# Two feed-forwards and a grouped attention in 512-wide and side-by-side passes

## The chip, the cores and the metric

One core of one Trainium2 chip runs the whole program: two transformer-like blocks, the second with two layers. The metric is the device time of one execution in microseconds, lower is better. A profiled execution adds a trace of every engine: TensorE (PE, and PEld for its weight loads), VectorE (DVE), ScalarE (ACT), GpSimd (POOL) and the queue of SyncE (SP), which issues the transfers.

## What is computed

The parts of the reference that the change touches, cut from the rest (all in fp32; 256 tokens, width 1024, hidden width 2816):

```python
def swiglu(hn, w_gate, w_up, w_down):
    return (jax.nn.silu(hn @ w_gate) * (hn @ w_up)) @ w_down
...
h = h + swiglu(rms_norm(h, ffn_norm_g[i]), w_gate[i], w_up[i], w_down[i])
...
def gqa_attend(q, k, v):
    s = jnp.einsum("bhgqd,bhkd->bhgqk", q, k).astype(jnp.float32) * (HEAD_DIM ** -0.5)
    p = jax.nn.softmax(s, axis=-1).astype(v.dtype)
    return jnp.einsum("bhgqk,bhkd->bhgqd", p, v)
...
def swiglu_2(h, w1, w3, w2):
    return (jax.nn.silu(h @ w1) * (h @ w3)) @ w2
```

The first block ends with one feed-forward (`swiglu`) for 256 tokens. The second block has two layers with two streams of 256 tokens each, the latent one and the context. In layer 0 both streams go through the attention and the feed-forward, 512 tokens in all; in layer 1 only the latent stream does, 256 tokens. The grouped attention has 8 query heads of 64 channels and 2 key and value heads; the latent stream attends to 512 keys, the context to its own 256.

## The kernel before, in words

Activations lie with channels on the partitions and tokens along the free axis. To keep fp32 accuracy, each operand is split in a high part (rounded to fp32r) and a low part (the rest), and a product is three passes into one PSUM tile: high by high, high by low, low by high. `mm3` (L282) issues them at L288, L289 and L290; each pass is a MATMUL with a weight load (LDWEIGHTS) of its own.

```python
nc.tensor.matmul(ps, lhsT=l[0], rhs=r[0], start=start, stop=False)
nc.tensor.matmul(ps, lhsT=l[0], rhs=r[1], start=False, stop=False)
nc.tensor.matmul(ps, lhsT=l[1], rhs=r[0], start=False, stop=stop)
```

A k-tile here is one stationary tile of 128 x 128 with its low part, applied to all tokens of the operand: three passes of 256 columns where there are 256 tokens.

Weights come from HBM in blocks of 128 output channels. `wload` (L266) issues one transfer of 512 KB into `wr`, then ACT casts it to the high part `wh` (L277) and VectorE subtracts to get the low part `wl` (the helper's line, L250). Each of the three has three buffers. `proj_fm` (L292) walks over groups of blocks that fill one PSUM tile of 512 columns, so two blocks share a tile when there are 256 tokens; three PSUM tiles (`pp`) rotate. When a group is complete its `evac` function takes the sums out.

`swiglu` (L1136) runs gate and up projections in pairs of blocks. `ev_g` and `ev_u` work on 512 columns at a time: tanh on ACT, two products on VectorE, and a split of the result into the high and low pages `G`. Then the down projection runs over 22 k-tiles for each of 8 blocks. `ffn1` (L1190) is the first block's feed-forward. Its first two pairs of blocks (the lead) run on the unnormalised operand `hr` while the norm is still being computed, and the factor `rbs` is multiplied in afterwards; the rest runs on `hf_hi` and `hf_lo`. `ffn2` (L1634) is the feed-forward of the second block; its operand pages are `H`, high and low apart.

`gqa` (L1375) computes for each of 4 pairs of heads and each stream the scores, the softmax `e` on ACT and VectorE, transposes of `e` (`pT`, split into `pt_hi` and `pt_lo`) and the sums over keys. There the values of both value heads are one stationary tile (`vh`, and `vl` for the low part), and of the 128 rows that come out only the 64 of the head in question are used.

The order of the work is set when the program is built. A scheduler sorts the instructions of each engine into one fixed order, from their dependencies and from the order in which the generators are woven; each engine then runs its list strictly in that order. Beside the feed-forward of the first block runs `ada` (L1254): products of modulation weights on VectorE (`aj`), whose steps `run` and `fill` (L1216) hand out between steps of the projection. Beside the grouped attention run the gating of another branch (`merge`) and the convolution (`conv`, on VectorE, `cy`).

Of the kernel before, what the change touches and what calls it, by code (L numbers as in the profile page):

```python
# [10 lines left out]
F32 = mybir.dt.float32  # L11
# [11 lines left out]
NF = FF // 128  # L23
# [157 lines left out]
class Prog:  # L181
# [146 lines left out]
    @staticmethod  # L328
    def tail(n_tok):

        per = 512 // n_tok
        g = [[(n + j, 0, 0, n_tok) for j in range(per)] for n in range(0, 6, per)]
        return g + [[(n, 0, t, t + 256)] for t in range(0, n_tok, 256) for n in (6, 7)]

# [854 lines left out]

    def ffn1(self, h, st, before_down):  # L1190

        t = self.t
        g = self.v("ffn_g")
        raw = self.scaled(h, g, "hr")
        rb = self.rs_bcast(st)
        hn = self.page("hf_hi", F32R), self.page("hf_lo", F32R)
        for k in range(8):
            s = slice(k * 256, k * 256 + 256)
            self.norm_apply(h[:, s], rb, g[:, k:k + 1], hn[0][:, s], hn[1][:, s])
        self.hold()  # L1200
        rbs = self.t512("rbs", F32, "h")[:, :256]
        self.nc.scalar.copy(rbs, rb)
        st = self.stats()
        st2 = self.stats(share=st)
        ev = self.ev_add(h, 0.5, st, (st2, self.v("fin_g")))
        pages = lambda ti, x, n: [(self.xpage if x == 0 or i == 0 else self.page)("G", F32R) for i in range(n)]
        self.run(self.swiglu(t["w_gate"], t["w_up"], lambda ti: [(t["w_downa"], 8), (t["w_downb"], 6)],
                             self.k256(hn), 256, pages, lambda ti, *a: ev(*a), [list(range(NF))], (self.k256(raw), rbs),
                             before_down), 0.5)
        return st  # L1210

# [130 lines left out]
    def values(self, l, at, n):  # L1342

        nc = self.nc
# [4 lines left out]
        for tt in range(4):  # L1349
            c = slice(tt * 128, tt * 128 + 128)  # L1350
            nc.tensor.transpose(ps[:, c], vz[:, c], self.ident)
        v = [self.kvp.tile([128, 512], F32R, tag="v" + x, bufs=2, name="v" + x) for x in "hl"]
# [22 lines left out]
    def gqa(self, l, at, qs, branch):  # L1375
# [6 lines left out]
        for n in range(4):  # L1382
# [3 lines left out]
            for i in qs:  # L1386
# [247 lines left out]
    def ffn2(self, l, hs, sts):  # L1634
        t = self.t
        last = l == 1
        qs = [0] if last else [0, 1]
        nq = 256 * len(qs)
        with ExitStack() as es:
            if not last:  # L1640
                self.extra(es, 4)
                self.ada_tiles(es, 1024, 2)
                self.bg = _seq(self.ada(0, 5, [0, 1]), *[self.ada(1, x, [0, 1] if x < 2 else [0]) for x in range(6)])
# [6 lines left out]
            thirds = [list(range(NF))] if last else [list(range(8)), list(range(8, 16)), list(range(16, 22))]  # L1650
# [3 lines left out]
            if last:  # L1654
                down = lambda ti: [(t[f"w2{l}a"], 8), (t[f"w2{l}b"], 6)]
            else:
                down = lambda ti: [(t[f"w2{l}a"][:, ti:ti + 1], 8)] if ti < 2 else [(t[f"w2{l}b"], 6)]
# [155 lines left out]
```

## Time and profile before

| | |
|---|---|
| median of 3 runs (lowest to highest) | 2183.4 us (2180.99 to 2183.92) |
| the profiled execution | 2183.66 us |
| its span | 2181.4 us |
| TensorE busy in the span | 2102.3 us |
| VectorE busy in the span | 1660.8 us |
| ScalarE busy in the span | 867.1 us |
| mean granted clock of TensorE | 0.985 |

Busy time is the time in which an engine had at least one instruction running. TensorE's passes overlap, so the distance between the starts of two passes says more about their price than the duration of one. A stretch of the table by windows gives the busy time of each engine in it; the engine that is close to the length of the stretch is the short one there.

### The profile page before, as it was taken

How to read it: one execution, taken by the hardware profiler on the slowest of the kernel's cores; microseconds unless marked ns; L12 is line 12 of the kernel's file. 1: busy time of each engine (PE TensorE's matmuls, PEld its weight loads, DVE VectorE, ACT ScalarE, POOL GpSimd, SP SyncE). 2: the span in 40 equal slices, each digit the busy share in tenths (PEclk: the TensorE clock that was granted, in tenths of full speed). 3: DMA queues.
4: the chain of work that ended last, by engine and by line, in shares of the span. 5: the costliest groups of instructions: out<-in, count | busy, mean ns of one | idle time of the engine just before them, and what ended most of it. 6: DMA issues, size and time to landing. Idle time of an engine off the chain costs nothing. (4 is left out here: it accounts for less than half of the span.)

```text
span 2181.4 us, 34428 instructions
## 1 busy us (share of the span) xinstructions
PE 2102.3 (96%) x13408; PEld 1838.3 (84%) x13408; DVE 1660.8 (76%) x3401; ACT 867.1 (40%) x1379; POOL 68.8 (3%) x92
## 2 busy tenths in 40 slices
PE   8898999999998999999999999999999989999998
PEld 7677999999987777777788888878898868999998
DVE  8987775886579998888875899763499977666554
ACT  2223354545433445445433322222245444444442
POOL 2350000000000000000000000000000000000000
PEclk9999999999999999999999999999999989999999
DMA  6227654475642212333455367752344313364553
GB/s 225 85 76 232 210 183 145 152 236 179 188 141 73 84 59 92 112 126 121 141 173 189 99 217 224 260 185 97 93 147 142 101 43 103 129 201 155 184 182 127
DMA packets 97826, 322.20 MB, mean 148 GB/s; under 512 B 10496, under 2 KB 16128, under 8 KB 96768
## 3 DMA queue, kind: packets, MB, share of 16 engines
q1 hardware_dynamic: 97664, 320.01, 45.6%
q8 instruction: 105, 1.72, 0.3%
q14 instruction: 57, 0.47, 0.1%
HBM read 315.78 MB, written 4.19 MB: 147 GB/s over the span
## 5 line engine op out<-in xcount | busy, mean ns | idle before, releaser
L277 ACT CAST wh<-wr 128x1024 fp32r<-128x1024 f32 (+2 forms) x455 | 470.4, 1034 | 786.3 <-PE pp L289 552.8
L250 DVE TENSOR_TENSOR wl<-wr,wh 128x1024 fp32r<-128x1024 f32 (+2 forms) x455 | 546.8, 1202 | 222.7 <-ACT wh L277 217.0
L288 PE MATMUL pp<-H,wh 128*128 128x512 f32 (+1 forms) x1648 | 566.5, 346 | 7.0 <-ACT H L450 3.7
L289 PE MATMUL pp<-H,wh 128*128 128x512 f32 (+1 forms) x1648 | 565.5, 345 | 0.7 <-DVE H L253 0.7
L290 PE MATMUL pp<-H,wl 128*128 128x512 f32 (+1 forms) x1648 | 563.9, 344 | 1.0 <-DVE wl L250 0.8
L288 PEld LDWEIGHTS pp<-H,wh 128*128 128x128 f32 x1648 | 314.2, 191 | 44.1 <-ACT H L450 4.3
L290 PEld LDWEIGHTS pp<-H,wl 128*128 128x128 f32 x1648 | 313.7, 191 | 36.6 <-DVE wl L250 2.0
L289 PEld LDWEIGHTS pp<-H,wh 128*128 128x128 f32 x1648 | 313.9, 191 | 35.3 <-issue 2.7
L1267 DVE SCALAR_TENSOR_TENSOR aj<-aw,silu 128x512 f32<-128x512 f32 x320 | 220.2, 688 | 54.9 <-DMA aw<-ada 50.5
L288 PE MATMUL pp<-G,wh 128*128 128x256 f32 (+1 forms) x540 | 170.3, 315 | 0.0
L290 PE MATMUL pp<-G,wl 128*128 128x256 f32 (+1 forms) x540 | 170.3, 315 | 0.0
L289 PE MATMUL pp<-G,wh 128*128 128x256 f32 (+1 forms) x540 | 170.2, 315 | 0.0
L253 DVE SCALAR_TENSOR_TENSOR cy<-U,vecs,cy 128x512 f32<-128x512 f32 (+1 forms) x240 | 147.3, 614 | 2.6
L288 PEld LDWEIGHTS pp<-G,wh 128*128 128x128 f32 x540 | 103.0, 191 | 6.5
L289 PEld LDWEIGHTS pp<-G,wh 128*128 128x128 f32 x540 | 103.0, 191 | 6.4
L290 PEld LDWEIGHTS pp<-G,wl 128*128 128x128 f32 x540 | 103.0, 191 | 6.3
L289 PE MATMUL pp<-hf_lo,wh 128*128 128x256 f32 x320 | 90.7, 284 | 1.0 <-DVE hf_lo L250 0.9
L290 PE MATMUL pp<-hf_hi,wl 128*128 128x256 f32 x320 | 90.5, 283 | 1.0 <-DVE wl L250 1.0
L288 PE MATMUL pp<-hf_hi,wh 128*128 128x256 f32 x320 | 90.7, 284 | 0.3 <-ACT hf_hi L447 0.3
L253 DVE SCALAR_TENSOR_TENSOR h<-pp,mod,h 128x256 f32<-128x256 f32 x80 | 35.6, 479 | 65.3 <-PE pp L290 61.9
L286 PE MATMUL pp<-xg,wf 128*128 128x256 f32 x320 | 76.4, 392 | 9.3 <-DVE th L250 7.4
L1110 ACT ACTIVATE e<-sc,st 128x512 f32<-128x512 f32 (+1 forms) x104 | 62.3, 604 | 45.0 <-DVE st L257 29.1
(501 smaller groups left out, 3855.7 us busy)
## 6 DMA issues: line engine op xcount, KB each, us to landing
wr<-w SPq DMA_DIRECT2D x88, 512.0 KB
aw<-ada SPq DMA_DIRECT2D x72, 512.0 KB
wr<-zg SPq DMA_DIRECT2D x64, 512.0 KB
wr<-wb SPq DMA_DIRECT2D x48, 512.0 KB
aw<-ada SPq DMA_DIRECT2D x48, 256.0 KB
wr<-w_gate SPq DMA_DIRECT2D x22, 512.0 KB
wr<-w_up SPq DMA_DIRECT2D x22, 512.0 KB
wr<-w_downa SPq DMA_DIRECT2D x16, 512.0 KB
```

What stands on the lines that cost most here:

```text
L250: (eng or self.nc.vector).tensor_tensor(out=out, in0=a, in1=b, op=op)
L253: self.nc.vector.scalar_tensor_tensor(out, a, s, b, op0, op1)
L277: nc.scalar.copy(hi, raw)
L286: nc.tensor.matmul(ps, lhsT=l, rhs=r, start=start, stop=stop)
L288: nc.tensor.matmul(ps, lhsT=l[0], rhs=r[0], start=start, stop=False)
L289: nc.tensor.matmul(ps, lhsT=l[0], rhs=r[1], start=False, stop=False)
L290: nc.tensor.matmul(ps, lhsT=l[1], rhs=r[0], start=False, stop=stop)
L1110: nc.scalar.activation(e, ps[:, x], AF.Exp, bias=st[:, 2 + x:3 + x], scale=scale, accum_out=st[:, 4 + x:5 + x])
L1267: nc.vector.scalar_tensor_tensor(junk, w[:, c:c + 512], 1.0, self.sc[s][:, b + c:b + c + 512], MUL, MUL, accum_out=raw[i][:, (b + c) // 51 ...
```

## The change

It does three things.

First, `proj_wide` and `swiglu_wide` take the place of `proj_fm` and `swiglu` in the feed-forward of the first block and in the one of layer 1. High and low parts of the operand lie side by side, 256 columns each (`hpair`). A k-tile is then two passes: the high weights by all 512 columns, and the low weights by the first 256. One block fills a PSUM tile, high and low sums side by side, and `added` puts them together: ACT copies one half into `sm`, VectorE adds the other. Tanh and products follow on `sm`, 512 wide for two blocks, and the split goes into pages `G` in which high and low parts of a block lie side by side. In the down projection `ev_wide` adds the two halves to `h` one after the other. The steps of `ada` are handed out at half the rate per step, since there are twice as many steps.

Second, in `gqa` the high and low values of one head lie side by side in one stationary tile (`vg`), so that two passes, `pt_hi` and `pt_lo`, give the high sums in 64 rows and the low sums in the other 64. After them a copy on ACT and an addition on VectorE for each head put the two together in `go`, and one split writes both heads. The product of low values with low probabilities, which was left out before, is in the sums now.

Third, `values` writes the tiles for that in two splits of half the size.

```diff
+    def proj_wide(self, parts, rhs, evac, blocks=None):
+        nc = self.nc
+        nt = parts[0][0].shape[3] // parts[0][1] // 128
+        for c in range(parts[0][0].shape[0]) if blocks is None else blocks:
+            w = [self.wload(src[c, b], kc) for src, kc in parts for b in range(src.shape[1])]
+            ks = [x for (src, kc), x in zip([p for p in parts for b in range(p[0].shape[1])], w) for x in
+                  [(x[0][:, k], x[1][:, k]) for k in range(kc)]]
+            for j in range(nt):
+                s = slice(j * 128, j * 128 + 128)
+                ps = self.ps("pp")
+                last = len(ks) - 1
+                for k, (h, l) in enumerate(ks):
+                    r = rhs(k)
+                    if k:
+                        nc.tensor.matmul(ps[:, :256], lhsT=l[:, s], rhs=r[:, :256], start=False, stop=False)
+                    nc.tensor.matmul(ps, lhsT=h[:, s], rhs=r, start=k == 0, stop=k == last)
+                    if not k:
+                        nc.tensor.matmul(ps[:, :256], lhsT=l[:, s], rhs=r[:, :256], start=False, stop=False)
+                evac(c * nt + j, ps.rearrange("p (x n) -> p x n", x=2))
+                yield
...
+    def swiglu_wide(self, gate, up, down, rhs, page, ev_down, lead=None, before_down=None):
+        nc = self.nc
+        G = [page(i) for i in range(-(-NF // 4))]
+        sums = {}
+        def added(which, f, pv, rb):
+            if f % 2 == 0:
+                sums[which] = self.t512("sm", F32, "g")
+            x = sums[which][:, f % 2 * 256:f % 2 * 256 + 256]
+            nc.scalar.copy(x, pv[:, 1])
+            self.tt(x, pv[:, 0], x, ADD)
+            if rb is not None:
+                self.tt(x, x, rb, MUL)
+            return sums[which]
+        def ev_g(f, pv, rb=None):
+            x = added(0, f, pv, rb)
+            if f % 2:
+                th = self.t512("th", F32, "h")
+                nc.scalar.activation(th, x, AF.Tanh, scale=0.5)
+                self.stt(x, th, 1.0, x, ADD, MUL)
+        def ev_u(f, pv, rb=None):
+            x = added(1, f, pv, rb)
+            if f % 2:
+                self.tt(x, x, sums[0], MUL)
+                g = G[f // 4].rearrange("p (f x n) -> p x f n", f=4, x=2)[:, :, f % 4 - 1:f % 4 + 1]
+                self.split(x.rearrange("p (f n) -> p f n", f=2), g[:, 0], g[:, 1])
+        for f in range(0, NF, 2):
+            r, rb = lead if f == 0 and lead else (rhs, None)
+            yield from self.proj_wide([(gate, 8)], r, lambda *a: ev_g(*a, rb=rb), [f, f + 1])
+            yield from self.proj_wide([(up, 8)], r, lambda *a: ev_u(*a, rb=rb), [f, f + 1])
+        if before_down:
+            before_down()
+        yield from self.proj_wide(down, lambda k: G[k // 4][:, k % 4 * 512:k % 4 * 512 + 512], ev_down)
...
+    def ev_wide(self, h, scale, sts):
+        def ev(n, pv):
+            s = slice(n * 256, n * 256 + 256)
+            c = scale if isinstance(scale, float) else scale[:, n:n + 1]
+            for x in range(2):
+                self.stt(h[:, s], pv[:, x], c, h[:, s], MUL, ADD)
+            if n % 2 or n >= 6:
+                for st, g in sts:
+                    self.ssq_add(st, h[:, (n if n >= 6 else n - 1) * 256:(n + 1) * 256], g)
+        return ev
...
     def values(self, l, at, n):
...
+        if n == 0:
+            out = []
+            for a, x in enumerate("hl"):
+                v = self.kvp.tile([128, 512], F32R, tag="v" + x, bufs=2, name="vg")
+                v4 = v.rearrange("p (t j c) -> p t j c", t=2, j=4)
+                self.split(ps[:, a * 256:a * 256 + 256].rearrange("p (t j c) -> p t j c", t=2, j=2), v4[:, :, 0::3], v4[:, :, 1:3])
+                out += [[v[:, o:o + 128] for o in (t, t + 128)] for t in (0, 256)]
+            return out
...
     def gqa(self, l, at, qs, branch):
...
-                        self.mm3(ov[:, j], tuple(x[:, kt * 128:kt * 128 + 128] for x in gv),
-                                 pt[m], m == 0, m == nk // 128 - 1)
+                        for x in range(2):
+                            nc.tensor.matmul(ov[:, j], lhsT=gv[kt][j], rhs=pt[m][x], start=m == x == 0,
+                                             stop=m == nk // 128 - 1 and x == 1)
                     yield
+                o = self.t512("go", F32, "h")[:, :256]
+                for j in range(2):
+                    rows, other = [slice(64 * x, 64 * x + 64) for x in (j, 1 - j)]
+                    nc.scalar.copy(o[rows], ov[other, j])
+                    self.tt(o[rows], ov[rows, j], o[rows], ADD)
                 c = slice(n * nq + i * 256, n * nq + i * 256 + 256)
-                for j in range(2):
-                    rows = slice(64 * j, 64 * j + 64)
-                    self.split(ov[rows, j], branch[0][rows, c], branch[1][rows, c])
+                self.split(o, branch[0][:, c], branch[1][:, c])
```

The order in which the engines run the instructions changes at three places that matter here. The names are those of the program with the number of the buffer.

VectorE (DVE) in the first feed-forward, behind the lead. `aj` are products of `ada`, `wl` are low parts of weights. Before, the end of the first pair and the split of the weights of the fourth block behind the lead:

```order
L1267 SCALAR_TENSOR_TENSOR aj_4427,ar_4419<-aw_4421,silu0_1711 128x512
L250 TENSOR_TENSOR gu_4407<-th_4342,pp_4345 128x512
L1267 SCALAR_TENSOR_TENSOR aj_4429,ar_4420<-aw_4421,silu1_1721 128x512
L253 SCALAR_TENSOR_TENSOR th_4492<-th_4492,pp_4431 128x512
L250 TENSOR_TENSOR G_4276<-gu_4407,G_4273 128x512
L250 TENSOR_TENSOR wl_4529<-wr_4526,wh_4528 128x1024
```

And now (the sums `pp_4417`, `pp_4443` and `pp_4471` are the first three blocks behind the lead):

```order
L250 TENSOR_TENSOR sm_4358<-sm_4358,sm_4302 128x512
L1348 SCALAR_TENSOR_TENSOR aj_4409,ar_4400<-aw_4401,silu1_1721 128x512
L250 TENSOR_TENSOR sm_4434<-pp_4417,sm_4434 128x256
L250 TENSOR_TENSOR G_4273<-sm_4358,G_4273 128x2x256
L250 TENSOR_TENSOR sm_4434<-pp_4443,sm_4434 128x256
L250 TENSOR_TENSOR sm_4488<-pp_4471,sm_4488 128x256
L250 TENSOR_TENSOR wl_4494<-wr_4491,wh_4493 128x1024
```

Three additions stand ahead of the same split, `wl_4494`, where none stood.

ScalarE (ACT) at the start of the last feed-forward, behind the last piece of the operand `H`. Before:

```order
L450 ACTIVATE H_19467<-nx_19513,mod1_3_0_14411 128x256
L277 CAST wh_19620<-wr_19618 128x1024
L277 CAST wh_19655<-wr_19653 128x1024
L1155 ACTIVATE th_19584<-pp_19523 128x512
L277 CAST wh_19685<-wr_19683 128x1024
```

And now:

```order
L473 ACTIVATE H_19036<-nx_19081,mod1_3_0_14032 128x256
L1223 COPY sm_19114<-pp_19097 128x256
L277 CAST wh_19173<-wr_19171 128x1024
L1223 COPY sm_19114<-pp_19123 128x256
L277 CAST wh_19201<-wr_19199 128x1024
```

A copy out of the sums of the first block (`pp_19097`) stands ahead of the cast of the fourth block's weights (`wh_19173`).

TensorE (PE) in the grouped attention of layer 0 (`o` are the sums of a head pair, `vh`, `vl` and `vg` the values, `pt_hi` and `pt_lo` the probabilities). Before, the end of one tile of keys, the next one, and what follows:

```order
L289 MATMUL o_7492<-pt_lo_7533,vh_7415 128x256
L290 MATMUL o_7492<-pt_hi_7532,vl_7416 128x256
L288 MATMUL o_7492<-pt_hi_7532,vh_7415 128x256
L289 MATMUL o_7492<-pt_lo_7533,vh_7415 128x256
L290 MATMUL o_7492<-pt_hi_7532,vl_7416 128x256
L289 MATMUL pp_8376<-H_5800,wh_8379 128x512
```

And now:

```order
L1152 MATMUL pT_7146<-ident_84,e_7130 128x128
L1487 MATMUL o_7102<-pt_lo_7143,vg_7023 128x256
L1487 MATMUL o_7102<-pt_hi_7142,vg_7023 128x256
L1487 MATMUL o_7102<-pt_lo_7143,vg_7023 128x256
L1487 MATMUL o_7102<-pt_hi_7151,vg_7026 128x256
L1127 MATMUL sc_7280<-kh_6913,qh_7030 128x256 x2
```

Each head of a tile of keys has two passes, by the high and by the low probabilities, where it had three.

## Rows read from the trace of the kernel before

**Rows 1.** The page's part 1: each engine's busy time, share, instructions.

```profile
PE 2102.3 (96%) x13408; PEld 1838.3 (84%) x13408; DVE 1660.8 (76%) x3401; ACT 867.1 (40%) x1379; POOL 68.8 (3%) x92
```

**Rows 2.** Busy time by stretch: length, PE, PEld, DVE, ACT, POOL, clock, DMA share, GB/s.

```profile
430.00:460.00 30.00, 30.00 (x252) 30.00 (x252) 28.52 (x55) 13.07 (x15) 0.00 (x0) 1.00 0.74 252
...
500.00:535.00 35.00, 35.00 (x294) 35.00 (x293) 25.97 (x36) 19.08 (x26) 0.00 (x0) 1.00 0.56 182
...
740.00:760.00 20.00, 17.98 (x100) 12.98 (x98) 19.90 (x46) 10.20 (x25) 0.00 (x0) 1.00 0.20 68
...
800.00:820.00 20.00, 19.03 (x84) 12.47 (x83) 19.52 (x31) 7.08 (x13) 0.00 (x0) 1.00 0.33 104
...
880.00:900.00 20.00, 19.57 (x102) 14.16 (x102) 17.55 (x37) 10.62 (x24) 0.00 (x0) 1.00 0.29 89
...
1420.00:1440.00 20.00, 19.62 (x85) 15.57 (x85) 16.20 (x38) 6.01 (x8) 0.00 (x0) 1.00 0.85 266
...
1760.00:1780.00 20.00, 16.15 (x70) 10.88 (x69) 16.72 (x47) 10.64 (x25) 0.00 (x0) 0.83 0.09 27
...
2020.00:2050.00 30.00, 30.00 (x252) 30.00 (x251) 17.59 (x19) 14.36 (x17) 0.00 (x0) 1.00 0.57 183
```

**Rows 3.** Groups by line and shape: busy us, mean ns | idle before.

```profile
L288 PE MATMUL pp<-G,wh 128*128 128x256 f32 x376 | 106.5, 283 | 0.0
...
L290 PE MATMUL pp<-hf_hi,wl 128*128 128x256 f32 x320 | 90.5, 283 | 1.0 <-DVE wl L250 1.0
...
L288 PE MATMUL o<-pt_hi,vh 128*128 128x256 f32 x80 | 26.7, 334 | 2.9 <-ACT pt_hi L262 2.6
...
L1267 DVE SCALAR_TENSOR_TENSOR aj<-aw,silu 128x512 f32<-128x512 f32 x320 | 220.2, 688 | 54.9 <-DMA aw<-ada 50.5
```

**Rows 4.** Timeline of PE: start us, duration; layer 0, then the last feed-forward.

```profile
1400.12 0.39 PE L288 MATMUL pp<-H,wh 128*128 128x512 f32 x1
...
1400.80 0.39 PE L288 MATMUL pp<-H,wh 128*128 128x512 f32 x1
...
2050.01 0.28 PE L288 MATMUL pp<-H,wh 128*128 128x256 f32 x1
...
2050.37 0.28 PE L288 MATMUL pp<-H,wh 128*128 128x256 f32 x1
```

**Rows 5.** Timeline of DVE around the start of the first feed-forward.

```profile
401.69 0.42 DVE L253 SCALAR_TENSOR_TENSOR hx<-pp,hx 128x256 f32<-128x256 f32 x1
402.02 0.41 DVE L250 TENSOR_TENSOR acc<-acc 128x256 f32<-128x256 f32 x1
...
418.36 1.23 DVE L250 TENSOR_TENSOR wl<-wr,wh 128x1024 fp32r<-128x1024 f32 x1 [0.21 <-ACT wh L277]
419.50 0.75 DVE L250 TENSOR_TENSOR hf_lo<-nx,hf_hi 128x256 fp32r<-128x256 f32 x2
...
421.11 0.82 DVE L250 TENSOR_TENSOR hf_lo<-nx,hf_hi 128x256 fp32r<-128x256 f32 x2
```

**Rows 6.** Timeline of PE there; in brackets its wait.

```profile
419.97 0.38 PE L289 MATMUL pp<-hf_lo,wh 128*128 128x256 f32 x1 [0.91 <-DVE hf_lo L250]
```

**Rows 7.** Timelines of PE, DVE and ACT at the start of the last feed-forward.

```profile
1977.84 0.79 PE L288 MATMUL pp<-H,wh 128*128 128x256 f32 x2 [1.11 <-ACT H L450]
...
1988.09 0.28 PE L288 MATMUL pp<-H,wh 128*128 128x256 f32 x1
...
1983.38 0.88 DVE L253 SCALAR_TENSOR_TENSOR H<-nx,mod,H 128x256 fp32r<-128x256 f32 x2 [0.18 <-ACT H L450]
...
1984.86 1.05 ACT L277 CAST wh<-wr 128x1024 fp32r<-128x1024 f32 x1 [1.11 <-issue]
```

**Rows 8.** Timeline of DVE at the end of the last feed-forward.

```profile
2169.73 0.48 DVE L253 SCALAR_TENSOR_TENSOR h<-pp,mod,h 128x256 f32<-128x256 f32 x1 [5.88 <-PE pp L290]
```

**Rows 9.** What works on the attention's sums: min/median/max ns.

```profile
L262 ACT CAST og_hi<-o x16: 359/367/369, 759.4 to 889.4; 64x256 fp32r<-64x256 f32 x16
L250 DVE TENSOR_TENSOR og_lo<-o,og_hi x16: 407/422/429, 759.8 to 890.2; 64x256 fp32r<-64x256 f32 x16
```

More of the change, by code (lines that the diff above doesn't have):

```diff
@@ L1188, in swiglu, with hpair @@
             yield from self.proj_fm(down(ti), r, n_tok, lambda *a: ev_down(ti, *a), groups=self.tail(n_tok) if last else None)
+    def swiglu_wide(self, gate, up, down, rhs, page, ev_down, lead=None, before_down=None):
[30 more added lines that the diff above has]
+        yield from self.proj_wide(down, lambda k: G[k // 4][:, k % 4 * 512:k % 4 * 512 + 512], ev_down)
+    def hpair(self, name, page=None):
+        x = [(page or self.page)(name, F32R) for _ in range(2)]
+        at = lambda k: x[k // 4][:, k % 4 * 512:k % 4 * 512 + 512]
+        return (lambda k: (at(k)[:, :256], at(k)[:, 256:])), at
     def ffn1(self, h, st, before_down):
@@ L1193, in ffn1 @@
         g = self.v("ffn_g")
-        raw = self.scaled(h, g, "hr")
+        nc = self.nc
+        parts, raw = self.hpair("hr")
+        for k in range(8):
+            x, (hi, lo) = h[:, k * 256:k * 256 + 256], parts(k)
+            nc.scalar.mul(hi, x, g[:, k:k + 1])
+            self.stt(lo, x, g[:, k:k + 1], hi.bitcast(F32), MUL, SUB)
         rb = self.rs_bcast(st)
-        hn = self.page("hf_hi", F32R), self.page("hf_lo", F32R)
+        parts, hn = self.hpair("hf")
         for k in range(8):
-            s = slice(k * 256, k * 256 + 256)
-            self.norm_apply(h[:, s], rb, g[:, k:k + 1], hn[0][:, s], hn[1][:, s])
+            self.norm_apply(h[:, k * 256:k * 256 + 256], rb, g[:, k:k + 1], *parts(k))
         self.hold()
-        rbs = self.t512("rbs", F32, "h")[:, :256]
-        self.nc.scalar.copy(rbs, rb)
+        rbs = self.t512("rbs", F32, "n")[:, :256]
+        nc.scalar.copy(rbs, rb)
         st = self.stats()
         st2 = self.stats(share=st)
[L1205 to L1209, printed above, removed]
-        return st
+        page = lambda i: (self.xpage if i < 4 else self.page)("G", F32R)
+        self.run(self.swiglu_wide(t["w_gate"], t["w_up"], [(t["w_downa"], 8), (t["w_downb"], 6)], hn, page,
+                                  self.ev_wide(h, 0.5, [(st, None), (st2, self.v("fin_g"))]), (raw, rbs), before_down), 0.25)
+        return st
+    def ev_wide(self, h, scale, sts):
[8 more added lines that the diff above has]
+        return ev
     def hold(self):
@@ L1637, in ffn2 @@
         qs = [0] if last else [0, 1]
+        if last:
+            parts, both = self.hpair("H")
+            self.norm_mod(l, 3, 0, hs[0], self.rs_bcast(sts[0]), lambda k, *_: parts(k))
+            st = self.stats()
+            _run(self.swiglu_wide(t[f"w1{l}"], t[f"w3{l}"], [(t[f"w2{l}a"], 8), (t[f"w2{l}b"], 6)], both,
+                                  lambda i: self.page("G", F32R), self.ev_wide(hs[0], self.mod[l, 5, 0], [(st, None)])))
+            return hs, [st]
         nq = 256 * len(qs)
         with ExitStack() as es:
[L1640 to L1643, printed above, removed]
+            self.extra(es, 4)
+            self.ada_tiles(es, 1024, 2)
+            self.bg = _seq(self.ada(0, 5, [0, 1]), *[self.ada(1, x, [0, 1] if x < 2 else [0]) for x in range(6)])
             at = self.hpages(nq)
@@ L1649, in ffn2 @@
             sts = [self.stats(("st", "tr")[i]) for i in qs]
-            thirds = [list(range(NF))] if last else [list(range(8)), list(range(8, 16)), list(range(16, 22))]
+            thirds = [list(range(8)), list(range(8, 16)), list(range(16, 22))]
             ev = self.ev_res(l, 5, hs, qs, sts)
@@ L1653, in ffn2 @@
             pages = lambda ti, x, n: [(self.xpage if ti == 1 else self.page)("G", F32R) for i in range(n)]
[L1654 to L1657, printed above, removed]
+            down = lambda ti: [(t[f"w2{l}a"][:, ti:ti + 1], 8)] if ti < 2 else [(t[f"w2{l}b"], 6)]
             self.run(self.swiglu(t[f"w1{l}"], t[f"w3{l}"], down, lambda k: at(k, 0, nq), nq, pages,
```

## The prediction

> **What bounds the kernel now.** I read the engine totals first [rows 1]: TensorE is busy 96% of the span, its weight loads 84%, VectorE 76%. So the end is set by TensorE's stream wherever VectorE keeps up, and the question of each stage is which of the two is short. The table of busy time by stretch [rows 2] answers it. In the first feed-forward (about 404 to 600 us) TensorE is busy all the time, but VectorE is not idle either: 28.52 of 30 us between 430 and 460, and 25.97 of 35 between 500 and 535. In the last feed-forward (about 1978 to 2170 us; the stretch from 2020) VectorE has 17.59 of 30, so nothing but TensorE is short. In the grouped attention of layer 0 (the stretches from 740 and 800) VectorE has 19.90 and 19.52 of 20 us and TensorE 17.98 and 19.03: VectorE, which also works off the convolution there, is as short as TensorE. At the end of that stage (from 880) it is TensorE again. In layer 1 (from 1760) both wait on each other, 16.15 and 16.72 of 20, at a granted clock of 0.83, a mean of the levels of 1.2 and 2.4 GHz.
>
> The groups by shape [rows 3] show what is touched: 256-column passes in the feed-forwards, and 80 passes of each of three kinds in the grouped attention (the row of one kind).
>
> **Price of a pass.** In the timeline of the last feed-forward three 256-column passes start 0.36 us apart as a set (2050.01 to 2050.37), 0.120 us each; 512-column passes of layer 0 start 0.68 us apart as three (1400.12 to 1400.80), 0.2267 us each [rows 4]. The 283 ns that a pass lasts [rows 3] overlap its neighbours; the start-to-start times are what counts. Twice 256 columns cost 0.240, once 512 0.2267, so joining two passes that share a stationary tile gives 13.3 ns: 0.360 us for one k-tile becomes 0.2267 + 0.120 = 0.3467.
>
> The Trainium skill, page "TensorE: Matmul & The Clock Gate", section "Back-to-back issue gap", gives the spacing of a pass at full clock as columns over 2.4 GHz plus about 2.5 ns. By it joining two passes would give only 2.5 ns, an estimate of 2.6 us for the 1056 k-tiles below. The rows show 13.3 ns more than the columns at either width, so they decide the sum; what a mixed stream does no row shows, and that is a rival below.
>
> **Part 1, feed-forwards, gross.** One feed-forward is 22 gate and 22 up blocks of 8 k-tiles and 8 down blocks of 22: 528 k-tiles. Two of them: 1056 x 13.3 ns = **14.1 us**, 7.05 each. Loads are the same in number and size. A block of weights (512 KB) is now wanted every 8 x 0.3467 = 2.77 us instead of 2.88, 189 GB/s; the stretch from 2020 shows 183 and that from 1420 shows 266 GB/s [rows 2], so I cost that at nothing.
>
> **What it adds.** Each gate or up block now brings an ACT copy of 256 columns and a VectorE addition of 256 columns, 44 of each per feed-forward; the silu work stays 512 wide per pair. A 256-column VectorE operation from PSUM lasts 0.42 us but holds the engine 0.33 (401.69 to 402.02) [rows 5]; 44 x 0.33 = 14.5 us. In the last feed-forward a pair of blocks then costs VectorE four weight splits of 1.14 (418.36 to 419.50) [rows 5], four additions and three 512-wide operations of about 0.6: 7.7 us against 4 x 2.77 = 11.1 of TensorE. Covered. In the first the ada work is in the same queue: from 430 on VectorE had 28.52 of 30 us, and with four additions for each of the 2.7 pairs in it that becomes 32. There it becomes short for a while, and what matters is what stands behind what.
>
> In VectorE's order after the change 18 rows stand between the last normalised operand (421.9 us [rows 5]) and the weight split of the fourth block after the lead, three of them additions that wait in line (shown with the diff): about 7.4 us by the same durations, so that split ends near 430.5, and TensorE wants it near 428.1. That is 2.4 us of waiting where before there was 1.0 [rows 3]. Following the rows on in the same way I find 0.1 and 0.8 us more in the next six blocks, and then VectorE leads again, since the ada rows stop after the eighth pair: 1.4 + 0.1 + 0.8 = 2.3, and I take 2.5 us. The lead itself gives nothing: TensorE already waits there for the normalised operand (0.91 us [rows 6]), whose last part is ready at the same 421.9, so the gain of these 40 k-tiles, 0.5 us, becomes waiting. The end, where every block now takes two 256-wide additions, is 0.4 later. First feed-forward: 7.05 - 2.5 - 0.5 - 0.4 = **3.6 us**.
>
> Start of the last feed-forward: TensorE begins at 1977.84 while VectorE still writes its operand until 1984.3 [rows 7]. Before, two blocks ran side by side, and the 73rd pass, the first after 24 k-tiles, began at 1988.09 [rows 7]. Now three blocks run side by side and the first pass needs both halves of the operand: the same 24 come out at about 1988.0, so their 0.3 us are not gained. The fourth block's weights can be cast only when the first block is through and its copy is taken (ACT's order, shown with the diff), so their split ends about 1988.9 and TensorE waits 0.6 for it. With 0.4 at the end (one more addition of 0.48 us, of which 0.4 holds the engine [rows 8]): 7.05 - 0.3 - 0.6 - 0.4 = **5.7 us**.
>
> **Part 2, grouped attention.** Of the 80 sets of three passes [rows 3] layer 0 has 48 (4 pairs of heads, 2 heads, 4 tiles of keys for the one stream and 2 for the other) and layer 1 has 32; each loses one of 0.120: 5.8 and 3.8 us gross. What is added per head pair and block of queries: two copies and two additions of 64 x 256, as long as the casts and subtractions they replace (0.37 and 0.42 [rows 9]), and one cast and one subtraction of 128 x 256; 0.34 us of VectorE each, 2.7 in layer 0, and 0.8 us on the chain to the result. The split of the values in halves adds under 0.5 us per layer. Where VectorE is short (740 to 820 [rows 2]) the removed passes buy nothing and the 0.34 counts; the later half of layer 0, where TensorE is short, keeps its gain. Bounds: the whole 5.8, or the 2.7 lost. I take **3 us**, the half for which the stretch from 880 speaks. Layer 1: bounds 3.8 (somewhat more at the lower clock) and -1; in the stretch from 1760 neither engine is full and a shorter chain helps in part: **2 us**.
>
> **Sum.** 3.6 + 5.7 + 3 + 2 = 14.3 us. The profiled execution took 2183.66 us, 0.26 over the median of the runs shown: 2183.66 - 14.3 = **2169.4 us**.
>
> **Rivals.**
> *All of it arrives.* Attention keeps 9.6 and VectorE's lag in the first feed-forward is hidden by its buffers: 2183.7 - 14.1 - 9.6 + 2.2 (lead, start and ends) = 2162.2. For it: three buffers of weights let VectorE run two blocks ahead. Against: 28.52 of 30. Chance 0.11.
> *Attention gives nothing.* What 740 to 820 shows holds for the whole stage, or the new order of the woven generators costs what the passes save: 2169.4 + 5 = 2174.4, and 2180 where the longer chains cost another 5. Chance 0.16.
> *The fixed share stays.* A 512-wide pass next to a 256-wide one costs its columns and keeps the overhead of the one that is gone (say a weight load that no longer hides): k-tiles stay at 0.360, the waits and ends cost 2.5 + 0.4 + 0.6 + 0.4 = 3.9 us, attention gives 5: 2182.6, no change. Against: at 256 columns the loads already follow each other at 0.120 us [rows 4], and the longer pass leaves more room. Chance 0.07.
> The Trainium skill's formula cited above ("TensorE: Matmul & The Clock Gate", "Back-to-back issue gap") would make it about 2180, an estimate with its 2.6 us; the spacings of [rows 4] speak against it.
> *Slower.* The split for block n+3 now stands behind the evacuation of block n and whatever ada rows are between. From the end of block n: copy 0.4, cast 1.05 [rows 7], split 1.14 and up to 5.3 us of other rows (four ada products of 0.69 [rows 3], three 512-wide operations, two additions) make 7.9 us against the 5.5 of two blocks: 2.4 us of waiting per pair, 26 us over 11 pairs. In place of my 2.5 that gives 2169.4 + 26.4 - 2.5 = 2193.3. It decides from 1.5 us per pair on (14.3 + 2.5 over 11 pairs), and from 1.9 it is more than 0.2% slower; I found 1.4, 0.1 and 0.8 in the first four pairs and none later. Chance 0.09.
>
> **Numbers.** The forecast keeps 0.57, with a range of its own of 2165 to 2176. The range to hold 8 in 10 takes in the full gain below and most of the case without attention above: 2160 to 2183; it leaves out the slower case and a few hundredths at either end. A measurement of this kernel tells about 0.2% (4.4 us) from nothing: faster is below 2179.0. Forecast 0.57, full 0.11 and 0.12 of the case without attention make 0.80 faster; the other 0.04 and the unchanged 0.07 make 0.11; slower 0.09.
>
> **What would show it.** Right: in the last feed-forward 24 k-tiles, 48 passes, in 8.32 us (72 passes in 8.64 before); 1136 passes fewer on TensorE and some 20 us less of busy time. In the first feed-forward waits of TensorE for weight splits (wl) of 2 to 4 us in all between 422 and 450 us, none in the last but at its start. In layer 0 the attention stage as long as before or 1 to 4 us shorter, with VectorE at 19 of 20. Wrong: waits for wl through all pairs; a spacing of 512 plus 256 columns over 0.350; attention stages longer than before.

## The result: 1.45% slower, with the time lost in the attention

The changed kernel took 2214.35 us (median of 4 runs, 2211.44 to 2215.99), the kernel before 2182.26 us beside it (4 runs). The ratio is 1.0145, 95% interval [1.0128, 1.0163]: 32 us slower where 14 us faster was forecast, and outside the range. TensorE is as busy as before (1.9 us more, where some 20 us less was forecast), and VectorE 51 us more ([rows 1] are the same line of before). The page of the changed kernel, parts 1 and 2; the last line is the clock row of before:

```profile
span 2211.0 us, 32423 instructions
...
PE 2104.2 (95%) x12272; PEld 1784.8 (81%) x12272; DVE 1712.0 (77%) x3524; ACT 900.2 (41%) x1481; POOL 68.6 (3%) x92
...
PEclk9999999999999899899999999999999879999999
...
PEclk9999999999999999999999999999999989999999
```

1136 passes are gone as forecast (13408 to 12272), and yet the busy time of TensorE has not fallen: it is measured in time, and the granted clock (PEclk) was down in four slices where before it was down in one. Busy time by stretch shows where. The columns are those of [rows 2]; the stretches are the first feed-forward with some 30 us of the next projection, the attention of layer 0, the attention of layer 1 and the last feed-forward, each from the same first instruction to the same last one. First before, then after:

```profile
404.20:629.10 224.90, 220.51 (x1814) 219.03 (x1812) 165.66 (x285) 106.68 (x141) 0.34 (x2) 0.99 0.59 189
700.00:1038.60 338.60, 331.88 (x1675) 255.26 (x1676) 296.76 (x682) 151.81 (x298) 0.00 (x0) 1.00 0.31 98
1646.30:1947.40 301.10, 291.54 (x2018) 257.22 (x2018) 240.41 (x506) 142.60 (x246) 0.00 (x0) 0.97 0.35 113
1977.80:2169.70 191.90, 191.87 (x1586) 191.83 (x1586) 108.65 (x123) 82.90 (x98) 0.00 (x0) 0.99 0.52 165
```

```profile
404.80:627.10 222.30, 217.00 (x1286) 189.92 (x1285) 183.30 (x342) 120.90 (x185) 0.34 (x2) 0.98 0.55 191
697.00:1048.10 351.10, 337.48 (x1627) 256.41 (x1628) 307.19 (x700) 154.45 (x307) 0.00 (x0) 0.96 0.28 96
1654.70:1979.30 324.60, 297.53 (x1985) 259.43 (x1986) 246.01 (x511) 144.43 (x251) 0.00 (x0) 0.93 0.30 104
2010.30:2198.90 188.60, 187.90 (x1058) 163.35 (x1058) 127.38 (x173) 96.22 (x141) 0.00 (x0) 0.99 0.49 168
```

The first stretch is 2.6 us shorter and the last one 3.3. Of the 2.6 only 1.0 lies in the first feed-forward itself, from its first pass to the one behind its last (before, then after):

```profile
404.24:599.26 195.02, 192.71 (x1597) 191.61 (x1596) 143.12 (x236) 93.00 (x120) 0.00 (x0) 1.00 0.60 195
...
404.80:598.85 194.05, 190.77 (x1070) 164.09 (x1069) 160.35 (x292) 106.87 (x164) 0.34 (x2) 0.98 0.57 195
```

The rest comes behind it: before, the granted clock fell to a mean of 0.66 for 5 us there, behind a wait of 2.1 us for the weights `wl`; after, the same wait (2.0 us) was followed by no fall.

```profile
618.00:623.00 5.00, 5.00 (x32) 5.00 (x31) 3.54 (x9) 1.05 (x1) 0.00 (x0) 0.66 0.65 209
```

The attention is 12.5 us longer in layer 0 and 23.5 us in layer 1, with lower clocks in both. What TensorE waited for in the grouped attention of layer 1, before and after (us in total, times, longest):

```profile
PE o L288 <- ACT pt_hi L262: 1.7, 3, 0.7
```

```profile
PE hb L1417 <- DVE hr L1414: 9.4, 2, 6.1
PE pT L1152 <- DVE e L257: 5.0, 2, 3.0
PE o L1487 <- ACT pt_hi L262: 3.0, 5, 0.7
PE hs L1404 <- ACT hq L1402: 1.6, 2, 0.8
```

`hq`, `hs`, `hr` and `hb` are the steps of `head_norm`, the norm of the query of the next pair of heads. Before, no wait of TensorE in this stretch is put down to them. ScalarE's timeline in layer 1 tells why. Before (start us, duration; `og<-o` takes out the finished sums of a pair):

```profile
1673.29 0.41 ACT L1321 ACTIVATE hq<-z 128x256 f32<-128x256 f32 x1
...
1698.77 0.37 ACT L262 CAST og<-o 64x256 fp32r<-64x256 f32 x1 [1.90 <-PE o L290]
...
1702.70 0.41 ACT L1321 ACTIVATE hq<-z 128x256 f32<-128x256 f32 x1
...
1725.36 0.37 ACT L262 CAST og<-o 64x256 fp32r<-64x256 f32 x1 [1.75 <-PE o L290]
...
1785.96 0.37 ACT L262 CAST og<-o 64x256 fp32r<-64x256 f32 x1 [0.28 <-PE o L290]
```

After (`go<-o` takes out the finished sums):

```profile
1704.56 0.37 ACT L1493 COPY go<-o 64x256 f32<-64x256 f32 x1
1704.83 0.41 ACT L1402 ACTIVATE hq<-z 128x256 f32<-128x256 f32 x1
...
1743.30 0.37 ACT L1493 COPY go<-o 64x256 f32<-64x256 f32 x1 [2.46 <-PE o L1487]
1743.57 0.41 ACT L1402 ACTIVATE hq<-z 128x256 f32<-128x256 f32 x1
...
1776.89 0.37 ACT L1493 COPY go<-o 64x256 f32<-64x256 f32 x1 [1.83 <-PE o L1487]
1777.17 0.41 ACT L1402 ACTIVATE hq<-z 128x256 f32<-128x256 f32 x1
...
1812.31 0.37 ACT L1493 COPY go<-o 64x256 f32<-64x256 f32 x1 [1.83 <-PE o L1487]
```

Before, the norm for the next pair begins 23 to 25 us ahead of the end of this pair's sums (1673.29 to 1698.77, 1702.70 to 1725.36), so it runs beside them. After, it begins 0.27 or 0.28 us behind the first copy into `go`, three times out of three. In layer 0 it is the same, 0.27 or 0.28 us behind the first copy of the pair's second stream (764.30 and 764.58, 817.84 and 818.11, 861.67 and 861.94). From the end of the first pair to the end of the fourth in layer 1 it was 87.2 us and is 107.8.

The theory that follows: `go` is `self.t512("go", F32, "h")`. Tag `h` has two buffers, and `hq`, `hr`, `hx` of `head_norm` and `rb` of `rope` take turns in them. With `go` as a fifth, the next `hq` and `hr` get their turn only when `go` has had its own, and `go` waits for the finished sums. The rivals are the longer way from the sums to the result, the fewer passes (less work to fill gaps), and a disturbance by the feed-forwards.

### The profile page after: what moved, and what is told of

Read it like the earlier page. It is cut to its first block, busy times and chain, and to the rows that moved or that the text cites. A ratio compares the mean times of both kernels' runs of the same rounds, so it can differ in the third digit from the quotient of the medians.

```text
span 2211.0 us, 32423 instructions
## 1 busy us (share of the span) xinstructions
PE 2104.2 (95%) x12272; PEld 1784.8 (81%) x12272; DVE 1712.0 (77%) x3524; ACT 900.2 (41%) x1481; POOL 68.6 (3%) x92
## 4 chain that ended last, share of the span: by engine, by line
PE 82%; DVE 12%; ACT 3%; DMA 2%; issue 1%; SPq 0%; DVEq 0%; ACTq 0%
PE pp L288 17%; PE pp L290 17%; PE pp L289 17%; PE pp L352 11%; PE pp L351 5%; PE pp L286 3%; DVE wl L250 2%; PE pT L1152 2%; PE sc L1127 2%; DVE cy L253 1%; PE o L1487 1%; ACT wh L277 1%; PE kk L697 1%; PE pt L286 1%; PE pp L354 1%
## 5 line engine op out<-in xcount | busy, mean ns | idle before, releaser
L288 PE MATMUL pp<-H,wh 128*128 128x512 f32 (+1 forms) x1296 | 467.9, 363 | 3.5 <-ACT H L473 2.6
L290 PE MATMUL pp<-H,wl 128*128 128x512 f32 (+1 forms) x1296 | 466.1, 361 | 0.8 <-DVE wl L250 0.6
L289 PE MATMUL pp<-H,wh 128*128 128x512 f32 (+1 forms) x1296 | 465.0, 360 | 0.7 <-DVE H L253 0.7
L288 PEld LDWEIGHTS pp<-H,wh 128*128 128x128 f32 x1296 | 246.6, 191 | 41.9 <-issue 3.8
L289 PEld LDWEIGHTS pp<-H,wh 128*128 128x128 f32 x1296 | 246.3, 191 | 34.6 <-issue 1.3
L352 PE MATMUL pp<-G,wh 128*128 128x512 f32 x352 | 123.2, 398 | 0.0
L352 PE MATMUL pp<-H,wh 128*128 128x512 f32 x352 | 121.5, 401 | 1.6 <-DVE H L253 1.6
L352 PE MATMUL pp<-hf,wh 128*128 128x512 f32 x320 | 112.0, 403 | 2.5 <-DVE sm L250 2.5
L351 PE MATMUL pp<-G,wl 128*128 128x256 f32 x336 | 94.3, 281 | 0.0
L1133 ACT ACTIVATE e<-sc,st 128x512 f32<-128x512 f32 (+1 forms) x104 | 62.2, 603 | 62.3 <-DVE st L257 50.9
L351 PE MATMUL pp<-H,wl 128*128 128x256 f32 x308 | 85.8, 281 | 0.0
L351 PE MATMUL pp<-hf,wl 128*128 128x256 f32 x280 | 78.8, 283 | 0.0
L352 PEld LDWEIGHTS pp<-G,wh 128*128 128x128 f32 x352 | 65.3, 188 | 14.8
L352 PEld LDWEIGHTS pp<-H,wh 128*128 128x128 f32 x352 | 63.6, 191 | 13.6 <-DVE H L253 1.9
```

The lines of the kernel that those rows point to most:

```text
L351: nc.tensor.matmul(ps[:, :256], lhsT=l[:, s], rhs=r[:, :256], start=False, stop=False)
L352: nc.tensor.matmul(ps, lhsT=h[:, s], rhs=r, start=k == 0, stop=k == last)
L1133: nc.scalar.activation(e, ps[:, x], AF.Exp, bias=st[:, 2 + x:3 + x], scale=scale, accum_out=st[:, 4 + x:5 + x])
```

## The experiments

### Which part

`ffn_only` is the changed kernel with the functions `gqa` and `values` of before; `gqa_only` is the kernel before with `gqa` and `values` of the change; the diff ahead shows both versions of each.

> The feed-forwards of the change with the grouped attention and its values as before. Theory (the loss sits in the attention: between the two traces the two attention stages are 36.2 us longer and the rest 6.6 us shorter): about 2175.5 us, 2173 to 2179, with the attention stages of both layers as long as before (339 and 301 us). Rival (the wide feed-forwards disturb the rest, by the order or by the clock): 2200 or more.

Measured: 2176.03 us, ratio 0.9967 [0.9954, 0.9980].

> The grouped attention and values of the change with the feed-forwards as before. Theory (loss in the attention alone): 2182.3 + 36 = about 2218 us, 2214 to 2223. Rival (the feed-forwards are to blame): 2175 to 2185.

Measured: 2223.39 us, ratio 1.0175 [1.0158, 1.0192]. The feed-forwards gain about 7 us alone, as expected; the attention alone loses 38 (0.0175 of 2184.7, the median of before in these runs). The rival that blames the feed-forwards falls.

### The place in the rotation

`place_only` puts one row into the kernel before, ahead of the two splits at the end of `gqa`; `place_own` puts the same element into a buffer of its own.

```diff
+                nc.scalar.copy(self.t512("go", F32, "h")[:1, :1], ov[:1, 1, :1])
```

```diff
+                nc.scalar.copy(self.kvp.tile([128, 256], F32, tag="go", bufs=1, name="go")[:1, :1], ov[:1, 1, :1])
```

> The kernel before, with its three passes and its own evacuation, and one thing more: behind each pair of heads a tile of the rotation of two that the norm and the rotary step of the next query use (tag h) is taken, and a single element is copied into it out of the finished sums. Theory (the new tile go stands in that rotation, so that the norm of the next pair of heads waits for the end of this pair's attention): nearly all of the loss comes without any other work, 2182.3 + 30 to 45 = 2212 to 2227 us, with the norm's passes (hs) behind the last sums of the pair before. Rival (the longer chain of copies and additions, or the fewer passes, changed the order and cost the time): 2181 to 2185.

Measured: 2220.04 us, ratio 1.0168 [1.0152, 1.0183].

> The kernel before with the same one-element copy out of the finished sums as in place_only, into a buffer of its own. Theory (the place in the rotation is what costs): as before, 2180 to 2186 us, attention stages 339 and 301 us. Rival (the copy itself: ScalarE's queue stands behind the finished sums): 2200 or more.

Measured: 2180.77 us, ratio 1.0000 [0.9989, 1.0011].

One element costs 1.7% in that rotation and nothing outside it. ScalarE's timeline of `place_only`:

```profile
1708.04 0.15 ACT L1399 COPY go<-o 1x1 f32<-1x1 f32 x1 [1.88 <-PE o L290]
...
1708.36 0.41 ACT L1321 ACTIVATE hq<-z 128x256 f32<-128x256 f32 x1
```

and what TensorE waits for in its layer 1:

```profile
PE hb L1336 <- DVE hr L1333: 9.9, 2, 6.8
PE pT L1129 <- DVE e L257: 5.0, 2, 3.0
```

The same place for `hq` and the same two waits as after the change (9.4 and 5.0), without its passes, copies or additions. The two attention stretches took 351.2 and 325.5 us in `place_only`, after the change 351.1 and 324.6, and in `place_own` 336.9 and 298.4. In `place_own` `hq` is ahead of the sums again:

```profile
1671.86 0.41 ACT L1321 ACTIVATE hq<-z 128x256 f32<-128x256 f32 x1
...
1697.30 0.15 ACT L1399 COPY go<-o 1x1 f32<-1x1 f32 x1 [1.88 <-PE o L290]
```

So the turn in the rotation is the cause, and the copy's wait on ScalarE is not. `go_own` and `go_n` are the whole change with `go` elsewhere: in one buffer of its own, and in tag `n`, which has two.

```diff
-                o = self.t512("go", F32, "h")[:, :256]
+                o = self.kvp.tile([128, 256], F32, tag="go", bufs=1, name="go")
```

```diff
-                o = self.t512("go", F32, "h")[:, :256]
+                o = self.t512("go")[:, :256]
```

> The whole change, with the tile go in a buffer of its own instead of the rotation of two that the norm uses. Theory (place in the rotation): the attention stages come back to before and keep about half of the 9.6 us of the passes removed, 2175.5 - 5 = about 2170 us, 2164 to 2176. Rival (longer chain to the result, or fewer passes that use up the work that fills the gaps): 2205 to 2215.

Measured: 2178.88 us, ratio 0.9978 [0.9968, 0.9989].

> The whole change with go in another rotation of two buffers that only the end of the convolution uses (tag n). Theory: as go_own, 2174 to 2179 us, since the norm's rotation is free again. Rival (go_own's single buffer held the next pair back): 2 to 4 us faster than go_own, 2171 to 2175.

Measured: 2179.22 us, ratio 0.9987 [0.9977, 0.9996].

Some 36 us (0.0167 of 2182) come back from one argument. `go_n` is no faster than `go_own`, so the single buffer does not hold the next pair back. But `go_own` missed its expectation (2176 at most) by 3 us: beside `ffn_only` (0.9967) the two-pass attention is no gain at all.

### Why two passes for three give nothing even so

`no_sum` takes `go` away and splits the high sums as before, so the products with the low values are computed but not in the result:

```diff
-                o = self.t512("go", F32, "h")[:, :256]
...
+                for j in range(2):
+                    rows = slice(64 * j, 64 * j + 64)
+                    self.split(ov[rows, j], branch[0][rows, c], branch[1][rows, c])
```

`third_pass` is `go_own` with the pass by the low probabilities run twice, so that their share counts double in the result.

```diff
-                        for x in range(2):
-                            nc.tensor.matmul(ov[:, j], lhsT=gv[kt][j], rhs=pt[m][x], start=m == x == 0,
-                                             stop=m == nk // 128 - 1 and x == 1)
+                        for y, x in enumerate((0, 1, 1)):
+                            nc.tensor.matmul(ov[:, j], lhsT=gv[kt][j], rhs=pt[m][x], start=m == y == 0,
+                                             stop=m == nk // 128 - 1 and y == 2)
```

> The whole change, but without go: the 64 rows of high sums of each head are split straight out of PSUM as before, so the products with the low values are computed and left out of the result. Theory V (with the rotation undone, layer 0 is bound by VectorE and the chain of the softmax, so the removed passes turn into waits): as go_own, 2174 to 2179 us, layer 0's attention 336 to 340 us. Theory E (the passes do save, and the copies, additions and the later split eat it): 2168 to 2173 us, 4 to 5 us of it in layer 0.

Measured: 2173.28 us, ratio 0.9958 [0.9943, 0.9973].

> go_own with three passes again for each tile of keys of a head: the one by the low probabilities runs twice, so their share counts double in the result. TensorE has as many passes as before, with everything else as in go_own. Theory V (what the removed passes saved in the grouped attention is given back, in waits and in a lower clock, since VectorE and the chain of the softmax set the end there): within 2 us of go_own, 2177 to 2181, with fewer and shorter drops of the clock in layer 0 (none before, 10 us in go_own). Rival (TensorE sets the end, so the removed passes were worth 0.120 us each and something else ate them): 2186 to 2190.

Measured: 2179.25 us, ratio 0.9994 [0.9985, 1.0004].

Four kernels differ in two things, the passes and what takes the sums out (`ffn_only` in `values` too), and their ratios, each to the kernel before of its own rounds, make a table: with the sums taken out as before, 0.9967 for three passes (`ffn_only`) and 0.9958 for two (`no_sum`); with copies and additions, 0.9994 for three (`third_pass`) and 0.9978 for two (`go_own`). So the copies and additions cost about 6 us with three passes (0.0027 of 2182, and the intervals do not touch) and 4 with two (0.0020), and the removed passes give 2 to 3.5 (0.0009 and 0.0016) of the 9.6 at which they were priced; the intervals of these last three differences overlap, so they are estimates. That is how the gain is given back: what takes the sums out costs as much as the passes save, or more.

No theory on record came out whole. V said that `third_pass` would be within 2 us of `go_own`: so by the medians (0.4 us apart), not by the ratios (3.5 us); its rival, 2186 to 2190, is further off. `no_sum` lies in E's range by the time, but E's 4 to 5 us in layer 0 are not there (336.8 us, `go_own` 338.6, `ffn_only` 337.1). V's other half, that the clock would fall less in `third_pass`, is wrong: it fell to 0.77 and 0.76 in the two stretches below, in `go_own` to 0.75 and 0.78.

The traces, one execution each, do not decide it. The two attention stretches together took 638.3 us in `ffn_only`, 638.3 in `go_own`, 639.1 in `go_n`, 636.1 in `no_sum` and 643.0 in `third_pass`; kernels with the attention of before lie between 635.3 (`place_own`) and 640.2 (`ada_late`, further down), and the traced execution of `third_pass`, at 2184.38 us, was the longest of its ten, 5.1 over their median.

Busy time by stretch in layer 0, 52 us (for `ffn_only` alone), 12 us and 10 us from the first `hs` on, in `ffn_only`, then `go_own`, then the 12 us in `third_pass`:

```profile
697.60:749.60 52.00, 51.95 (x255) 41.09 (x255) 50.30 (x108) 18.23 (x31) 0.00 (x0) 1.00 0.24 82
749.60:761.60 12.00, 9.17 (x55) 6.75 (x55) 11.81 (x25) 6.13 (x15) 0.00 (x0) 1.00 0.25 88
761.60:771.60 10.00, 10.00 (x54) 7.76 (x53) 9.11 (x18) 3.43 (x6) 0.00 (x0) 1.00 0.12 40
```

```profile
751.50:763.50 12.00, 7.06 (x32) 4.69 (x33) 11.58 (x24) 5.80 (x16) 0.00 (x0) 0.75 0.26 88
763.50:773.50 10.00, 10.00 (x44) 8.51 (x44) 7.84 (x15) 2.42 (x6) 0.00 (x0) 0.78 0.01 2
```

```profile
754.00:766.00 12.00, 7.62 (x39) 5.55 (x38) 10.94 (x23) 5.14 (x15) 0.00 (x0) 0.77 0.24 88
```

In the first 52 us TensorE is full (51.95) and VectorE nearly so (50.30), and most of TensorE's passes are projections. In the next 12 TensorE is busy 9.17 us in `ffn_only` and keeps 2.4 GHz (1.00); in `go_own` it is busy 7.06, in `third_pass` 7.62, and the clock is at 1.2 GHz for a part of the time (means of 0.75 and 0.77). `third_pass` falls with the passes of before, behind the new copies and additions: its longest wait in these 12 us is 1.7, for the addition into `go`. For `go_own` the two rows give at most (1 - 0.75) x 12 + (1 - 0.78) x 10 = 5.2 us lost to the clock.

But the fall does not belong to the new attention. `ada_late` has the attention of before in this place, is busy 9.40 us in the same 12, more than `ffn_only`, and falls as well:

```profile
744.40:756.40 12.00, 9.40 (x46) 7.23 (x46) 11.11 (x23) 5.48 (x14) 0.00 (x0) 0.75 0.25 88
756.40:766.40 10.00, 10.00 (x53) 8.17 (x52) 8.71 (x16) 3.97 (x7) 0.00 (x0) 0.95 0.01 2
```

So does `no_sum`, which has no copies and additions (0.66). And with the attention of before the stretch of layer 0 took 338.8 us in `ada_late`, with the fall, and 336.9 to 338.6 in the kernel before, `ffn_only` and `place_own`, without it. So neither what sets the clock off here nor how much of the gain it takes is shown.

### The feed-forwards

In the first feed-forward VectorE's order put `ada` (`aj`) ahead of the additions that free the PSUM tiles. VectorE's timeline of the changed kernel:

```profile
426.24 0.70 DVE L1348 SCALAR_TENSOR_TENSOR aj<-aw,silu 128x512 f32<-128x512 f32 x1
...
427.45 0.70 DVE L1348 SCALAR_TENSOR_TENSOR aj<-aw,silu 128x512 f32<-128x512 f32 x1
...
428.06 0.43 DVE L250 TENSOR_TENSOR sm<-pp,sm 128x256 f32<-128x256 f32 x1
```

TensorE's longest wait from 417 to 437 us, and the busy time in three stretches of gate and up behind the lead:

```profile
PE pp L352 <- DVE sm L250: 2.5, 2, 2.4
```

```profile
417.40:428.20 10.80, 8.87 (x49) 7.23 (x48) 10.72 (x34) 7.69 (x15) 0.00 (x0) 1.00 0.27 97
428.20:435.00 6.80, 6.01 (x16) 4.42 (x17) 6.79 (x12) 0.90 (x2) 0.00 (x0) 0.50 0.53 179
435.00:536.80 101.80, 101.24 (x577) 87.67 (x577) 89.58 (x157) 58.46 (x90) 0.00 (x0) 1.00 0.62 215
```

TensorE waits 2.4 us for the addition at 428.06, and then runs at half clock for 6.8 us. `ada_late` (on `ffn_only`) starts `ada` later, and then hands it out faster:

```diff
-        self.run(self.swiglu_wide(t["w_gate"], t["w_up"], [(t["w_downa"], 8), (t["w_downb"], 6)], hn, page,
...
+        gen = self.swiglu_wide(t["w_gate"], t["w_up"], [(t["w_downa"], 8), (t["w_downb"], 6)], hn, page,
...
+        for i, _ in enumerate(gen):
+            self.fill(0.35 if i >= 10 else 0)
```

> ffn_only, with the first step of ada in the first feed-forward handed out after the 10th block instead of at once (rate 0.35 for 0.25). Theory (the 2.4 us wait at 426 to 429 us comes from the ada rows ahead of the additions that free the PSUM tiles, and the clock fell to half for 6.8 us right behind it): wait and drop both go, gate and up of the first feed-forward take 114.5 to 116 us for 119.4, and the whole 3 to 5 us less than ffn_only: 2171 to 2173. Rival (the wait is the additions' own): as ffn_only within 1 us.

Measured: 2167.13 us, ratio 0.9935 [0.9918, 0.9952]. Gate and up behind the lead took 112.2 us instead of 119.4, without a wait and at full clock. That is more than the 3.4 to 4.9 us expected, and the whole lies below the 2171 to 2173 expected:

```profile
417.70:529.90 112.20, 112.20 (x641) 97.47 (x640) 106.09 (x202) 66.65 (x106) 0.00 (x0) 1.00 0.62 215
```

The other open size was the spacing. `pair_order` (on `go_n`) lets the passes follow as high, low, low, high:

```diff
-                    if k:
+                    if k % 2:
...
-                    if not k:
+                    if k % 2 == 0:
```

> go_n with the two passes of a k-tile in alternating order, so that two 512-wide or two 256-wide passes follow each other (high, low, low, high). After the change a k-tile takes 0.3494 us in gate and up and 0.353 in down where 0.3467 was forecast. Theory (the price sits where the width changes): 0.348 to 0.350 in both and 1.5 to 3 us less than go_n. Rival (it belongs to each wide pass of this stream): spacing and time as go_n, within 1 us.

Measured: 2177.90 us, ratio 0.9977 [0.9966, 0.9988], beside 0.9987 for `go_n`; the intervals overlap. TensorE's timeline in the last down projection, `go_n` first:

```profile
2119.78 0.40 PE L352 MATMUL pp<-G,wh 128*128 128x512 f32 x1
2120.01 0.28 PE L351 MATMUL pp<-G,wl 128*128 128x256 f32 x1
...
2121.90 0.40 PE L352 MATMUL pp<-G,wh 128*128 128x512 f32 x1
```

```profile
2119.95 0.63 PE L352 MATMUL pp<-G,wh 128*128 128x512 f32 x2
...
2121.34 0.63 PE L352 MATMUL pp<-G,wh 128*128 128x512 f32 x2
```

Six k-tiles in 2.12 us are 0.353 each; four in 1.39 are 0.348. The down projection took 62.2 and 61.5 us, and over the 176 k-tiles that is 0.3534 and 0.3494, in the range of the theory. In gate and up, where it expected the same, nothing was gained (behind the lead of the first feed-forward 119.0 us in `go_n` and 119.1 in `pair_order`). So the order of widths has a part, but a k-tile stays over the 0.3467 worked out from streams of one width; why is open.

### What beats both

`both` is `ada_late` with the alternating order, the two edits shown above; `both_l1` adds the two-pass attention, with `go` in a buffer of its own, in layer 1 alone (`gqa0` is the function of before, `gqa1` that of `go_own`):

```diff
+    def gqa(self, *a):
+        return (self.gqa0, self.gqa1)[a[0]](*a)
...
-        if n == 0:
+        if n == 0 and l == 1:
```

> ada_late with the alternating order of passes of pair_order: 1.4 us less in the two down projections than ada_late by the 0.7 us each that pair_order's trace showed; 2169 to 2172. Rival: no difference.

Measured: 2166.55 us, ratio 0.9936 [0.9918, 0.9954].

> both, with the two-pass grouped attention in layer 1 alone (go in a buffer of its own), where go_own's stages were 3.4 us shorter up to the merge of the convolution and 1.4 us in all. Theory (in layer 1 a part of the gain stays): 1 to 2 us less than both. Rival (as in layer 0 it comes back as waits and clock): within 0.5 us of both or slower.

Measured: 2168.20 us, ratio 0.9940 [0.9925, 0.9956].

`ada_late`, `both` and `both_l1` can't be told apart, so neither the 1.4 us of the order nor a gain in layer 1 is shown by the times. They are 0.6% faster than the kernel before and 2.1% faster than the changed one, and two of them have the attention as it was.

## Why the prediction was wrong, point by point

**Grouped attention: the step that failed.** Part 2 priced what is added by the durations of its rows ("0.34 us of VectorE each", "0.8 us on the chain to the result") and bounded the loss by VectorE's 2.7 us in layer 0 and 1 us in layer 1. It did not count that `go` takes a buffer, and from which rotation. The line stood in the diff; the users of tag `h` in `head_norm` and `rope` were not taken into account, and no rival had them either. In place of 5 us gained the attention gave 36 lost, and `place_only` shows that the turn alone, without any of the change's work, costs as much.

**The passes removed.** Taken at 5 us of 9.6, with what is added counted in; with the rotation freed (`go_own`, `go_n`) the attention gains nothing that the traces or ratios tell. By the ratios the passes give 2 to 3.5 us, and the copies and additions cost 4 to 6. "Where VectorE is short the removed passes buy nothing" is not shown: in the first 52 us of layer 0 TensorE is as full as VectorE. The lower clock behind them was in no term of the sum. A gain of nothing was a rival (0.16), priced at 2174.4 to 2180; `go_own`, which is not the kernel that was forecast, came to 2178.88.

**Price of a k-tile.** Forecast 0.3467 us, measured 0.350 in gate and up (112.20 us for 320 in `ada_late`, 0.3506) and 0.3534 in down (62.2 for 176). By these the gross gain is 704 x 9.4 ns + 352 x 6.6 ns = 8.9 us, not 14.1. The sign named for this, a spacing over 0.350, is there. The Trainium skill's formula ("TensorE: Matmul & The Clock Gate", "Back-to-back issue gap") gives joining two passes 2.5 ns, but that section calls it the gap of an isolated pass, and the streams here load weights for each pass; the measured 9.4 and 6.6 lie between that and my 13.3.

**First feed-forward.** Forecast 3.6 us, measured 1.0 (195.02 to 194.05). Two terms were off. The gross 7.05 were 4.5 by the spacing above (352 x 9.4 ns + 176 x 6.6 ns). And behind the lead the 320 k-tiles of gate and up took 118.8 us before, 3.6 over 320 x 0.360, and 119.4 after, 7.2 over 320 x 0.3506: 3.6 us more lost, where 2.5 were forecast; 4.5 - 3.6 = 0.9. The mechanism, VectorE's additions and `ada` rows in line behind the lead, was right in part: a wait of 2.4 us came where 2.4 was worked out. But it was for the addition that frees a PSUM tile; waits for `wl`, for which the 2.4 was worked out, were 0.7 us in the whole feed-forward, so that the numbers agree is luck. What the sum left out is the half clock for 6.8 us behind the wait, 3.4 us. In the later pairs one wait of 0.6 us comes, so the slower rival (2.4 us per pair) did not occur, and the measured 2214 has nothing to do with it.

**Last feed-forward.** Forecast 5.7 us, measured 3.3, or 2.9 with the 0.4 at the end (from the last pass on: 11.7 us before, 12.1 after). The wait for the fourth block's weights at the start was forecast at 0.6 us and is this row:

```profile
PE pp L354 <- DVE wl L250: 0.7, 1, 0.7
```

No other wait came in the stretch but the one for the operand at its start (1.6 us, before 1.1). The shortfall is the spacing: 7.05 us gross were 4.5 (352 x 9.4 ns + 176 x 6.6 ns).

## What to carry to other kernels

A new tile is priced by its place as well as by its instructions: list who else takes turns in its buffers, in program order, and ask whose next turn now waits for this tile's producer. A tile that is written at the end of a stage does not belong in a rotation that the start of the next stage uses. And where the work taken off TensorE leaves it waiting, look at the granted clock behind each new wait (0.50 for 6.8 us in the first feed-forward) before counting the gain.

## What was not expected of the hardware

A wait of 2.4 us in the first feed-forward was followed by 6.8 us at 1.2 GHz, so the wait cost 2.4 + 3.4 us. A wait does not always do that: one of 2.0 us behind that feed-forward left the clock at 1.00, and before the change the same one, 2.1 us, was followed by a mean of 0.66 for 5 us. In the 12 us of layer 0 shown above the clock stayed at 1.00 with TensorE busy 9.17 us in one kernel, and fell to a mean of 0.75 with 9.40 in another. In a stream that mixes 512 and 256 columns, a pair of passes took 0.348 to 0.353 us by place and order, where streams of one width give 0.2267 + 0.120 [rows 4].
